# One expert layer in bf16 on one core: all of x loaded in float32 by SyncE and cast on chip

## The chip, the cores and the metric

The kernel runs on one NeuronCore of a Trainium2 chip. The core has five engines with instruction streams of their own: TensorE (PE, matmuls), VectorE (DVE), ScalarE (ACT), GpSimd (POOL, called Pool here) and SyncE (SP). [...] Data moves between the device memory and the on-chip SBUF by 16 DMA engines, which serve transfers that SyncE or Pool has issued. The metric is the device time of one execution in microseconds (us); lower is better.

## The reference

```python
n_experts, capacity, hidden, expert_hidden = 8, 256, 512, 2048

def reference(x, w1, w2):          # all float32
    h = np.matmul(x, w1)           # (8,256,512) @ (8,512,2048)
    h = np.maximum(h, 0)
    return np.matmul(h, w2).astype(np.float32)   # (8,256,2048) @ (8,2048,512)
```

Eight experts, each with its own tokens and weights: two matmuls with a ReLU between them. x is 4.19 MB, w1 and w2 are 33.55 MB each in float32.

## The kernel before, in words

**Data.** Weights are cast to bf16 by the DMA transfers that load them, into four slots each of `w1_sb` and `w2_sb` (slot = expert modulo 4). x is kept in bf16 in `x_sb`, which is the place of slot 2 of `w2_sb`: 16 rows of 512 elements per partition (`R` = 16, `H` = 512). TensorE turns it into `xT` by 64 transposes, and only then may the weights of slot 2 be loaded there.

**Order.** The kernel uses a Tile context only for its beginning. There, in a critical section (L135), SyncE issues one float32 transfer of the first four rows of x (`HEAD` = 4, L136) into the output buffer `out_sb`, which is free until the first expert is done. Then the context is closed (L137) and compiled, and everything after it is written out engine by engine with waits on the kernel's own semaphores:

- SyncE (L140 to L149) waits for each weight load in turn and counts it for TensorE (`c_w1`, `c_w2`). At the end it stores the last expert's output (L145).
- Pool (L152 to L201) issues the other twelve rows of x as one casting transfer (L153), makes the identity for the transposes (L154, L157), then issues all weight loads (L190): experts 0 and 1 of w1, the same of w2, experts 2 and 3 of w1, and so on. From the fourth on, each waits until its slot has been used; the fourth, w2 of experts 2 and 3, waits for all transposes (L171). A small output transfer (L181) goes ahead of the last half load of weights, and the output of experts 0 to 6 is issued behind the weights (L193).
- VectorE (L212 to L228) waits for the head of x (`d_head`), casts it into `x_sb` (L214), then moves half of the transposes from PSUM to `xT` (L206) and later the outputs from PSUM to `out_sb` (L225).
- ScalarE (L231 to L245) moves the other half of the transposes (L206), applies the ReLU (L239) and evicts the last output block (L245).
- TensorE waits for the cast, the identity and the rest of x (L323 to L325), runs the transposes (L328) and then a loop over the eight experts (L444): 64 matmuls into `h_ps`, in which each expert first takes its w1 count (L410), then 32 into `o_ps`, which take the w2 counts in two halves (L414). The helper of L99 takes a count, and all matmuls stand on L275.

The waits and the order of the lines are written by hand; no scheduler moves them.

Of the kernel before, what the change touches and what calls it, by code (L numbers as in the profile page):

```python
# [16 lines left out]
def kernel(  # L17
# [7 lines left out]
    nc = tc.nc  # L25
    P = 128
    E, C, H = x.shape
    F = w1.shape[2]
    MC = C // P
# [2 lines left out]

    R = E * C // P

    HEAD = 4

    NS = 4

# [10 lines left out]
    x_v = x.rearrange("e (pp r) k -> (e pp) (r k)", r=R)  # L49
# [7 lines left out]
    def allot(name, shape, dtype):  # L57
        nonlocal free
        places[name] = free
        t = nc.alloc_sbuf_tensor_at(name, shape, dtype, offset=free)  # L60
        free += math.prod(shape[1:]) * mybir.dt.size(dtype)
        return t


    out_sb = allot("out_sb", [P, E, MC, H], FP32)
# [7 lines left out]
    x_sb = w2_sb[:, 2, :]  # L73
# [8 lines left out]
    def sem(name):  # L82
        s = nc.alloc_semaphore(name)
        sems.append(s)
        return s

    d_last, d_pool = sem("d_last"), sem("d_pool")
# [3 lines left out]
        for w, slots in [(1, (0, 2, 3)), (2, (0, 1, 2, 3))]  # L91
        for i in slots
    }
    d_head, d_half = sem("d_head"), sem("d_half")
    s_event, s_cast, s_stored = sem("s_event"), sem("s_cast"), sem("s_stored")
    s_pe, v_last = sem("s_pe"), sem("v_last")

# [3 lines left out]
    def after_transposes(n):  # L101
        return s_pe, n

    def after_hidden(e, groups):
        return s_pe, K1 * MC + e * (NG + MC) + groups

    def after_outputs(e, halves):
        return s_pe, K1 * MC + e * (NG + MC) + NG + halves
# [22 lines left out]

    x_head = out_sb[:, :HEAD // MC].rearrange("p e m h -> p (e m h)")
    with tc.tile_critical(no_gpsimd_drain=True):  # L135
        nc.sync.dma_start(x_head, x_v[:, :HEAD * H]).then_inc(d_head, 16)  # L136
    tc.close()  # L137
    tc.compile()  # L138

# [1 line left out]
    for i, (w, es, h, n) in enumerate(loads):  # L141
# [8 lines left out]


    pool = nc.gpsimd  # L152
    pool.dma_start(x_sb[:, HEAD * H:], x_v[:, HEAD * H:]).then_inc(d_pool, 16)  # L153
    pool.memset(identity[:], 0.0).then_inc(s_event)  # L154
    pool.wait_ge(s_event, 1)

# [6 lines left out]
        pattern=[[-1, P]],  # L163
        channel_multiplier=1,
    ).then_inc(s_event)
    for i, (w, es, h, n) in enumerate(loads):


        old = es[-1] - NS
        if w == 2 and 2 in es:  # L170
            pool.wait_ge(*after_transposes(K1 * MC))  # L171
        if old >= 0 and h == 0:
            if w == 1:
                pool.wait_ge(*after_hidden(old, NG))
            else:
                pool.wait_ge(*after_outputs(old, MC))
        if i == len(loads) - 1:


            pool.wait_ge(s_event, 3)  # L180
            pool.dma_start(  # L181
                out_v[:16, 0, :16], out_sb[:16, 0, 0, :16]
            ).then_inc(d_pool, 16)
        e, ne, at_slot = es[0], len(es), es[0] % NS
        if w == 2:
            src = w2_v[:, e:e + ne, h:h + n, :].rearrange("p e h n -> p e (h n)")
            dst = w2_sb[:, at_slot:at_slot + ne, h * JH * H:(h + n) * JH * H]
        else:
            src, dst = w1_v[:, e:e + ne, :], w1_sb[:, at_slot:at_slot + ne, :]
        pool.dma_start(dst, src).then_inc(landed[i][0], 16)  # L190
    pool.wait_ge(s_event, 4)
    pool.wait_ge(d_pool, 32)
    pool.dma_start(  # L193
        out_v[:, :E - 1, :], out_sb[:, :E - 1].rearrange("p e m h -> p e (m h)")
    ).then_inc(d_pool, 16)
    pool.wait_ge(s_stored, 1)
    pool.wait_ge(d_pool, 48)
    used = [s.num for s in sems[1:]]
    used = range(min(used), max(used) + 1)
    pool.dma_reset(used)  # L200
# [9 lines left out]


    dve = nc.vector  # L212
    dve.wait_ge(d_head, 16)
    dve.tensor_copy(x_sb[:, :HEAD * H], x_head).then_inc(s_cast)  # L214
    dve.sem_inc(c_xt[0], 1)
    for ko in range(K1):
        dve.wait_ge(*after_transposes(ko * MC + 1))
# [11 lines left out]


    act = nc.scalar  # L231
    act.sem_inc(c_xt[1], 1)
    for ko in range(K1):
        act.wait_ge(*after_transposes(ko * MC + 2))
# [15 lines left out]
    pe = nc.tensor  # L250
# [42 lines left out]
    def last_column(step):  # L293

        return (P - 1) * step * 2
# [24 lines left out]
                i += 1  # L320
            t.then_inc(s_pe)

    pe.wait_ge(s_cast, 1)  # L323
    pe.wait_ge(s_event, 2)
    pe.wait_ge(d_pool, 16)  # L325
    x_first = X_AT + last_column(K1)
    pe.reg_mov(reg["x"], x_first)
    loop("transposes", reg["x"], x_first + K1 * 2, transposes)  # L328
# [146 lines left out]
```

## Time and profile before

| what | us |
|---|---|
| median of 3 runs | 179.47 |
| lowest and highest run | 179.31, 180.14 |
| the profiled execution's own time | 180.34 |
| its span, from the first to the last instruction | 179.0 |
| busy in that span: TensorE matmuls | 126.7 |
| ScalarE, VectorE, Pool | 38.7, 15.8, 10.9 |

The profile is of one execution. A timeline row has the start, the duration, the engine, the line, the operation with the tiles it writes and reads, and in brackets the idle time before it with what ended it; "q" behind an engine is its sequencer, which waits and issues transfers. A row of the stretches has the stretch, its length, the busy time of TensorE matmuls, TensorE weight loads, VectorE, ScalarE and Pool with counts, the granted clock, the share of the 16 DMA engines, and the GB/s written; a packet counts where it starts.
The queue that Pool issues to is called q0 (software_dynamic), SyncE's is q1 (hardware_dynamic).

### The profile page before, as it was taken

Reading aid. Unit: us, or ns where it says so; the run is one execution under the profiler, and the core shown is the slowest. Engines: PE = TensorE matmul, PEld = TensorE weight load, DVE = VectorE, ACT = ScalarE, POOL = GpSimd, SP = SyncE. Lnnn points to the kernel's source line nnn. Section 1 sums busy time; section 2 is a strip of 40 time slices with the busy share of each in tenths; the row PEclk is TensorE's granted clock in tenths of the full one; section 3 lists DMA queues with packets and bytes.
Section 4 is the critical chain, followed back from the end, with each engine's and each line's share of the span. In section 5 each row is a group of like instructions: output and inputs, shape, how many; then the busy total and the mean of one; then the engine's idle time right before and its main releaser. Section 6 shows DMA issues by size and latency. Waiting matters only on the chain. (4 is left out here: it accounts for less than half of the span.)

```text
span 179.0 us, 2075 instructions
## 1 busy us (share of the span) xinstructions
PE 126.7 (71%) x824; PEld 89.7 (50%) x832; DVE 15.8 (9%) x20; ACT 38.7 (22%) x38; POOL 10.9 (6%) x21
## 2 busy tenths in 40 slices
PE   0007630695029999993059999999999999959980
PEld 0006520585014695593023795695596497449530
DVE  0203420000000200200000200200110020020010
ACT  2002420044000063044000062053044044005310
POOL 3600010000000002101000101100020000001000
PEclk9999999999557999999657999999999999999999
DMA  5999989999999999999999998999999999999997
GB/s 185 253 207 231 227 190 231 227 194 223 231 209 205 227 216 201 231 216 198 231 220 194 231 223 190 231 227 194 223 231 205 209 234 216 198 212 218 303 421 310
DMA packets 3744, 40.37 MB, mean 226 GB/s; under 512 B 288, under 2 KB 288, under 8 KB 1312
## 3 DMA queue, kind: packets, MB, share of 16 engines
q0 software_dynamic: 3456, 38.80, 97.5%
q1 hardware_dynamic: 288, 1.57, 2.4%
HBM read 71.30 MB, written 4.20 MB: 422 GB/s over the span
## 5 line engine op out<-in xcount | busy, mean ns | idle before, releaser
L275 PE MATMUL o_ps<-w_sb,hT 128*128 x248 | 59.8, 396 | 19.6 <-PEq L99 18.8
L275 PE MATMUL h_ps<-xT,w_sb 128*128 x512 | 60.9, 281 | 11.3 <-PEq L99 11.3
L275 PEld LDWEIGHTS h_ps<-xT,w_sb 128*128 x512 | 57.7, 146 | 15.4 <-issue 12.0
L239 ACT ACTIVATE hT<-h_ps 128x1024 bf16<-128x1024 f32 x32 | 32.8, 1024 | 110.2 <-PE h_ps L275 110.2
L275 PEld LDWEIGHTS o_ps<-w_sb,hT 128*128 128x128 bf16 x256 | 25.5, 101 | 51.2 <-issue 24.7
L225 DVE COPY out_sb<-o_ps 128x512 f32<-128x512 f32 x15 | 9.7, 686 | 140.3 <-PE o_ps L275 140.3
L275 PE MATMUL xt_ps<-identity,w_sb 128*128 128x128 bf16 x64 | 7.6, 311 | 16.2 <-PEq L99 16.2
L275 PEld LDWEIGHTS xt_ps<-identity,w_sb 128*128 x64 | 6.5, 146 | 16.9 <-issue 16.9
L190 POOL DMA_DIRECT2D w_sb<-in_w_dram x12 | 8.0, 667 | 104.2 <-PE h_ps L275 56.9
L206 ACT COPY xT<-xt_ps 128x1024 bf16<-128x1024 bf16 x4 | 4.0, 1012 | 17.0 <-PE xt_ps L275 17.0
L206 DVE COPY xT<-xt_ps 128x1024 bf16<-128x1024 bf16 x4 | 4.9, 1224 | 12.2 <-PE xt_ps L275 12.2
L193 POOL DMA_DIRECT2D out_dram<-out_sb x1 | 1.0, 964 | 33.2 <-DMA out_dram<-out_sb 33.2
L245 ACT COPY out_sb<-o_ps 128x512 f32<-128x512 f32 x1 | 0.6, 586 | 5.9 <-PE o_ps L275 5.9
L206 ACT ACT_TABLE_LOAD x1 | 1.3, 1283 | 2.4 <-PEq L138 2.4
L214 DVE CAST w_sb<-out_sb 128x2048 bf16<-128x2048 f32 x1 | 1.2, 1227 | 5.8 <-DMA out_sb<-in_x_dram 5.8
L181 POOL DMA_DIRECT2D out_dram<-out_sb x1 | 0.5, 512 | 14.7 <-DVEq L228 14.7
L153 POOL DMA_DIRECT2D w_sb<-in_x_dram x1 | 0.7, 682 | 2.4 <-POOLq L138 2.4
L157 POOL TENSOR_SCALAR_AFFINE_SELECT identity<-identity 128x128 bf16<-128x128 bf16 x1 | 0.3, 284 | 0.2 <-POOL identity L154 0.2
L154 POOL MEMSET identity<- 128x128 bf16 x1 | 0.2, 224 | 0.0
L459 POOL MEMSET const-float32-0.0<- 128x1 f32 x1 | 0.1, 93 | 0.2 <-issue 0.2
L459 POOL MEMSET const-bfloat16-1.0<- 128x1 bf16 x1 | 0.1, 96 | 0.0
L459 POOL MEMSET const-uint8-127<- 128x1 uint8 x1 | 0.1, 96 | 0.0
(1 smaller groups left out, 0.1 us busy)
## 6 DMA issues: line engine op xcount, KB each, us to landing
w_sb<-in_w_dram POOLq DMA_DIRECT2D x5, 4096.0 KB, 47.1
w_sb<-in_w_dram POOLq DMA_DIRECT2D x5, 2048.0 KB, 51.2
out_dram<-out_sb POOLq DMA_DIRECT2D x1, 3584.0 KB, 12.9
w_sb<-in_w_dram POOLq DMA_DIRECT2D x2, 1024.0 KB, 43.3
w_sb<-in_x_dram POOLq DMA_DIRECT2D x1, 1536.0 KB, 10.6
out_sb<-in_x_dram SPq DMA_DIRECT2D x1, 1024.0 KB, 4.9
out_dram<-out_sb SPq DMA_DIRECT2D x1, 512.0 KB, 4.7
out_dram<-out_sb POOLq DMA_DIRECT2D x1, 1.0 KB, 33.7
```

The lines of the kernel that those rows point to most:

```text
L153: pool.dma_start(x_sb[:, HEAD * H:], x_v[:, HEAD * H:]).then_inc(d_pool, 16)
L157: pool.affine_select(out=identity[:], in_=identity[:], compare_op=mybir.AluOpType.not_equal, fill=1.0, base=0, pattern=[[-1, P]], channel_ ...
L181: pool.dma_start(out_v[:16, 0, :16], out_sb[:16, 0, 0, :16]).then_inc(d_pool, 16)
L190: pool.dma_start(dst, src).then_inc(landed[i][0], 16)
L193: pool.dma_start(out_v[:, :E - 1, :], out_sb[:, :E - 1].rearrange("p e m h -> p e (m h)")).then_inc(d_pool, 16)
L206: return copy(xT[:, ko, m].rearrange("k (ep r2) -> k ep r2", r2=R // MC), xt_ps[m][:].rearrange("k r2 ep -> k ep r2"),)
L214: dve.tensor_copy(x_sb[:, :HEAD * H], x_head).then_inc(s_cast)
L225: cp = dve.tensor_copy(out_sb[:, e, m, :], o_ps[m][:])
L239: act.activation(hT[:, g * GJ:(g + 1) * GJ, :].rearrange("p a c -> p (a c)"), h_ps[g % UG][:], mybir.ActivationFunctionType.Relu,).then_in ...
L245: act.copy(out_sb[:, E - 1, 1, :], o_ps[1][:]).then_inc(v_last)
L275: return pe.add_instruction(inst)
L459: nc = _bacc.Bacc("TRN2", target_bir_lowering=False, num_devices=1)
```

## The change

Three transfers by SyncE, of rows 0 to 3, 4 to 9 and 10 to 15, bring all of x in float32 into `out_sb`. They stand in the Tile context without a critical section, and each is put on the context's list of instructions that get none of its own semaphores. Each has a semaphore of the kernel, `d_x[0]` to `d_x[2]`. VectorE casts rows 0 to 3, 4 to 9 and 10 to 13, each when it has landed; ScalarE casts rows 14 and 15; TensorE waits for all four casts. Pool no longer loads x; its first weight load waits for `d_x[1]`, the first ten rows. Counts on `d_pool` at the end become one transfer smaller.

```diff
--- before.py
+++ after.py
@@ -32,7 +32,7 @@
 
     R = E * C // P
 
-    HEAD = 4
+    HEAD, BODY = 4, 10
 
     NS = 4
 
@@ -91,7 +91,7 @@
         for w, slots in [(1, (0, 2, 3)), (2, (0, 1, 2, 3))]
         for i in slots
     }
-    d_head, d_half = sem("d_head"), sem("d_half")
+    d_x, d_half = [sem(f"d_x{i}") for i in range(3)], sem("d_half")
     s_event, s_cast, s_stored = sem("s_event"), sem("s_cast"), sem("s_stored")
     s_pe, v_last = sem("s_pe"), sem("v_last")
 
@@ -131,9 +131,16 @@
 
 
 
-    x_head = out_sb[:, :HEAD // MC].rearrange("p e m h -> p (e m h)")
-    with tc.tile_critical(no_gpsimd_drain=True):
-        nc.sync.dma_start(x_head, x_v[:, :HEAD * H]).then_inc(d_head, 16)
+
+    x_f32 = out_sb[:].rearrange("p e m h -> p (e m h)")
+
+    def rows(a, b):
+        return slice(a * H, b * H)
+
+
+    for i, (a, b) in enumerate([(0, HEAD), (HEAD, BODY), (BODY, R)]):
+        load = nc.sync.dma_start(x_f32[:, rows(a, b)], x_v[:, rows(a, b)]).then_inc(d_x[i], 16)
+        tc.info.no_tile_sem_insts.add(load.ins.name)
     tc.close()
     tc.compile()
 
@@ -150,7 +157,6 @@
 
 
     pool = nc.gpsimd
-    pool.dma_start(x_sb[:, HEAD * H:], x_v[:, HEAD * H:]).then_inc(d_pool, 16)
     pool.memset(identity[:], 0.0).then_inc(s_event)
     pool.wait_ge(s_event, 1)
 
@@ -163,6 +169,7 @@
         pattern=[[-1, P]],
         channel_multiplier=1,
     ).then_inc(s_event)
+    pool.wait_ge(d_x[1], 16)
     for i, (w, es, h, n) in enumerate(loads):
 
 
@@ -189,12 +196,12 @@
             src, dst = w1_v[:, e:e + ne, :], w1_sb[:, at_slot:at_slot + ne, :]
         pool.dma_start(dst, src).then_inc(landed[i][0], 16)
     pool.wait_ge(s_event, 4)
-    pool.wait_ge(d_pool, 32)
+    pool.wait_ge(d_pool, 16)
     pool.dma_start(
         out_v[:, :E - 1, :], out_sb[:, :E - 1].rearrange("p e m h -> p e (m h)")
     ).then_inc(d_pool, 16)
     pool.wait_ge(s_stored, 1)
-    pool.wait_ge(d_pool, 48)
+    pool.wait_ge(d_pool, 32)
     used = [s.num for s in sems[1:]]
     used = range(min(used), max(used) + 1)
     pool.dma_reset(used)
@@ -210,8 +217,17 @@
 
 
     dve = nc.vector
-    dve.wait_ge(d_head, 16)
-    dve.tensor_copy(x_sb[:, :HEAD * H], x_head).then_inc(s_cast)
+    SPLIT = 14
+
+    def cast(copy, a, b):
+        return copy(x_sb[:, rows(a, b)], x_f32[:, rows(a, b)])
+
+    dve.wait_ge(d_x[0], 16)
+    cast(dve.tensor_copy, 0, HEAD).then_inc(s_cast)
+    dve.wait_ge(d_x[1], 16)
+    cast(dve.tensor_copy, HEAD, BODY).then_inc(s_cast)
+    dve.wait_ge(d_x[2], 16)
+    cast(dve.tensor_copy, BODY, SPLIT).then_inc(s_cast)
     dve.sem_inc(c_xt[0], 1)
     for ko in range(K1):
         dve.wait_ge(*after_transposes(ko * MC + 1))
@@ -229,6 +245,8 @@
 
 
     act = nc.scalar
+    act.wait_ge(d_x[2], 16)
+    cast(act.copy, SPLIT, R).then_inc(s_cast)
     act.sem_inc(c_xt[1], 1)
     for ko in range(K1):
         act.wait_ge(*after_transposes(ko * MC + 2))
@@ -320,9 +338,8 @@
                 i += 1
             t.then_inc(s_pe)
 
-    pe.wait_ge(s_cast, 1)
     pe.wait_ge(s_event, 2)
-    pe.wait_ge(d_pool, 16)
+    pe.wait_ge(s_cast, 4)
     x_first = X_AT + last_column(K1)
     pe.reg_mov(reg["x"], x_first)
     loop("transposes", reg["x"], x_first + K1 * 2, transposes)
```

## What was predicted, before the changed kernel was run

> **What bounds the kernel now.** I read the page first: its second and third parts, for which resource is never idle.
>
> ```profile
> span 179.0 us, 2075 instructions
> DMA  5999989999999999999999998999999999999997
> GB/s 185 253 207 231 227 190 231 227 194 223 231 209 205 227 216 201 231 216 198 231 220 194 231 223 190 231 227 194 223 231 205 209 234 216 198 212 218 303 421 310
> q0 software_dynamic: 3456, 38.80, 97.5%
> q1 hardware_dynamic: 288, 1.57, 2.4%
> ```
>
> The sixteen DMA engines are full from the first slice to the last (each slice is 4.5 us). Pool's queue (q0) takes 97.5% of them, SyncE's (q1) 2.4%. TensorE cannot be the bound where it waits for weights, so next the timeline, for its waits and the end:
>
> ```profile
> 32.93 9.89 PE L275 MATMUL h_ps<-xT,w_sb 128*128 x64 [9.21 <-PEq L99]
> 159.41 7.31 PE L275 MATMUL h_ps<-xT,w_sb 128*128 x64 [2.08 <-PEq L99]
> 166.61 7.07 PE L275 MATMUL o_ps<-w_sb,hT 128*128 x31
> 173.71 0.59 ACT L245 COPY out_sb<-o_ps 128x512 f32<-128x512 f32 x1 [5.93 <-PE o_ps L275]
> 174.32 0.35 SPq L145 DMA_DIRECT2D out_dram<-out_sb  x1
> ```
>
> Line 99 is TensorE taking a count that SyncE gives when a weight load has landed. TensorE stands 9.21 us before its first weights, and again 2.08 us before the last expert's. From there the rest is fixed work: 14.3 us of matmuls to 173.7, the eviction, the last store. So the end moves with the stream of weights one for one, and the stream moves with the moment at which x is through the DMA engines. Anything that TensorE does before 32.93 has 9.21 us of cover. The change is therefore worth what it does to the stretch ahead of the weights. That stretch, from the timeline, with one row of a narrower timeline for Pool's third weight issue and the page's times to landing:
>
> ```profile
> 0.35 0.10 POOL L459 MEMSET const-uint8-127<- 128x1 uint8 x1
> 0.95 0.38 SPq L136 DMA_DIRECT2D out_sb<-in_x_dram  x1
> 2.83 0.68 POOL L153 DMA_DIRECT2D w_sb<-in_x_dram  x1 [2.38 <-POOLq L138]
> 4.41 2.80 POOL L190 DMA_DIRECT2D w_sb<-in_w_dram  x3 [0.15 <-issue]
> 5.83 1.23 DVE L214 CAST w_sb<-out_sb 128x2048 bf16<-128x2048 f32 x1 [5.83 <-DMA out_sb<-in_x_dram]
> 13.95 1.89 PE L275 MATMUL xt_ps<-identity,w_sb 128*128 128x128 bf16 x16 [13.95 <-PEq L99]
> 24.03 0.72 POOL L190 DMA_DIRECT2D w_sb<-in_w_dram  x1 [16.82 <-PE xt_ps L275]
> ```
>
> ```profile
> 5.87 1.33 POOL L190 DMA_DIRECT2D w_sb<-in_w_dram  x1
> ```
>
> ```profile
> w_sb<-in_x_dram POOLq DMA_DIRECT2D x1, 1536.0 KB, 10.6
> out_sb<-in_x_dram SPq DMA_DIRECT2D x1, 1024.0 KB, 4.9
> ```
>
> And its DMA rates by stretch (last two columns: share of the DMA engines, GB/s written), then two answers on single stretches: the weights from 12.2 to 167.6 us, and the big float32 store from 173 to 175.4 us:
>
> ```profile
> 1.00:2.00 1.00, 0.00 (x0) 0.00 (x0) 0.00 (x0) 0.00 (x0) 0.00 (x0) 1.00 0.10 16
> 2.00:3.00 1.00, 0.00 (x0) 0.00 (x0) 0.00 (x0) 0.59 (x1) 0.17 (x1) 1.00 0.86 197
> 3.00:4.00 1.00, 0.00 (x0) 0.00 (x0) 0.00 (x0) 0.69 (x1) 0.76 (x3) 1.00 0.99 418
> 4.00:5.00 1.00, 0.00 (x0) 0.00 (x0) 0.00 (x0) 0.00 (x0) 0.85 (x2) 1.00 1.16 438
> 11.00:12.00 1.00, 0.00 (x0) 0.00 (x0) 0.00 (x0) 0.00 (x0) 0.00 (x0) 1.00 0.93 197
> 12.00:13.00 1.00, 0.00 (x0) 0.00 (x0) 0.00 (x0) 0.00 (x0) 0.00 (x0) 1.00 1.29 270
> ```
>
> ```profile
> DMA packets 2399, 33.55 MB, mean 216 GB/s; under 512 B 224, under 2 KB 224, under 8 KB 224
> ```
>
> ```profile
> DMA packets 249, 1.02 MB, mean 425 GB/s; under 512 B 0, under 2 KB 0, under 8 KB 249
> ```
>
> The lesson is in the last two: a transfer that casts float32 to bf16 writes 216 GB/s, so it reads 432; a plain float32 one moves 425. The engines pay for the float32 side either way.
>
> **The change, part by part.** x has 1,048,576 elements, 4.19 MB in float32, in 16 rows per partition.
>
> *Twelve rows leave Pool's casting transfer for SyncE's float32 ones.* Before, they write 1.57 MB: 1.57 / 0.216 = 7.28 us of the DMA engines. After, they move 3.15 MB: 3.15 / 0.425 = 7.40 us. Price +0.12 us. Bounds: at the 438 of the 4:5 row 7.18 us (-0.10), at its neighbour's 418 7.53 us (+0.25).
>
> *SyncE issues outside a section.* It now does so at 0.95 us, after the section's entry. Every engine is held at a start-up barrier that cannot end before Pool's last constant memset (0.35 + 0.10 = 0.45). Without the section the first issue falls between 0.45 and 0.95; I take 0.75, since the barrier's own signals stay: -0.20 us (bounds -0.50 and 0). The second and third issue cost SyncE 0.38 us each, while the first transfer is still moving. They also delay the end-of-context barrier, where Pool, VectorE and ScalarE arrive, by less than a microsecond; Pool's identity is not used until the transposes.
>
> *When x is through.* The rows 1:2 to 4:5 hold 1.07 MB by 5.0 us, so by 4.8 after the change. The other 3.12 MB at 425 take 7.35 us: the last packets start at about 12.15. Before, the same count gives 5.0 + 1.55 / 0.216 = 12.2.
>
> *Pool's weights wait for ten rows (d_x[1]).* This is the new wait. All weight loads stand behind it in Pool's queue; before, the first three were issued from 4.41 to 7.21, some 5 us ahead of need. Ten rows are 2.62 MB: 1.55 MB beyond the 1.07, 3.65 us, so 8.45. From the end of the bytes to the semaphore the head needed 5.83 - 5.0 = 0.83 us, so the wait ends at 9.3. VectorE starts at the same moment, on the same semaphore, its second cast: 3072 columns at 1.23 us for 2048 make 1.84 us, to 11.15. What that does to Pool is in the rows: the first two weight issues take from 4.41 to 5.87, 0.73 each; the third, issued while the cast runs, takes 1.33 and ends at 7.20, which is 0.14 after the cast's end at 7.06. So I let Pool's first issue end 0.14 after the cast: 11.3, not 9.3 + 0.73 = 10.05.
>
> [...]
>
> From the end of an issue to the first packet I need the body of x: issued by 2.83 + 0.68 = 3.51. These rows are for 2.83 to 4.79 us, then 4.5 to 5.5:
>
> ```profile
> q1 hardware_dynamic: 99, 0.81, 98.5%
> ```
>
> ```profile
> q0 software_dynamic: 16, 0.20, 105.6%
> q1 hardware_dynamic: 42, 0.21, 51.1%
> ```
>
> Pool's packets appear at 4.8, as SyncE's run out: at most 1.3 us after the issue's end, and perhaps much less, since they may have stood behind the head. So the first weight packets come between 11.3 and 12.6, where x runs out at 12.15. The gap in the stream is 0 to 0.45 us. I take 0, the value that the handover at 4.8 is nearest to. If Pool cannot begin its issue at all until the cast ends, it is 11.15 + 0.73 + 1.3 = 13.2, a gap of up to 1.05.
>
> *Casts and transposes.* The last rows land at 12.15 + 0.83 = 13.0; VectorE casts four rows (1.23 us) beside ScalarE's two, so TensorE may begin 0.5 us after 14.2, at about 14.7 instead of 13.95. Transposes end, and Pool's fourth weight issue goes, 0.8 us later than 24.03. The cover is the 9.21 us before 32.93, and three loads of 4 MB already queued. Price 0; gone only if x landed some 8 us later still. The casts stand on engines that do nothing else then.
>
> *Waits renumbered at the end, one fewer Pool transfer*: no work on the path.
>
> **The sum:** -0.20 + 0.12 + 0 = -0.08 us. The profiled execution took 180.34 us, its span 179.0; the median of the runs is 179.47. The difference applies to each, so 179.4 us.
>
> **The rivals.**
>
> *The cast starves Pool's descriptors, and the DMA engines run dry between x and the weights.* This one ends slower. It decides when the first weight packet comes after 12.15; every 0.1 us beyond goes into the time. At the bound from rows, 13.2, the sum is -0.08 + 1.05 = +0.97: 180.4 us; half-way, 179.9. For it: Pool's third issue was stretched by 0.6 us by a cast a third shorter. Against: x's last 1.5 MB cover 3.7 us of the wait.
>
> *Each of SyncE's transfers starts slowly, as the first did.* Row 2:3 moved 197 where 425 was possible: 0.54 us lost. Twice more is +1.1: 180.5 us. Against it: the head handed over to the body within 4.5 to 5.5, and the body to the weights within 11 to 13, without such a dip, though those were other queues. [...]
>
> *The weights' packets mix with the last part of x.* Then x lands later, up to some microseconds, and the transposes with it. The bytes are the same and the cover holds: 179.4 us. For it: two queues with work at once. Against it, from 174.3 to 176 us, after SyncE's store was issued at 174.32:
>
> ```profile
> q0 software_dynamic: 176, 0.72, 102.9%
> ```
>
> No packet of SyncE's is among them, so a queue that is deep may go first.
>
> *The change does not bring SyncE's issue forward*, because something other than the section holds it at 0.95: +0.12, 179.6 us.
>
> **How the numbers follow.** A measurement of this kernel can tell about 0.5%, 0.9 us, from no change: faster means under 178.6, slower over 180.4. Chances: forecast 0.58; starved Pool 0.16, of which 0.06 at its upper end or beyond; slow starts 0.08, nearly all of it slower; mixed queues 0.12; no earlier start 0.06. A gain of 0.9 would need more than every favourable bound: -0.50 - 0.10 = -0.60 us. I leave it 0.05 out of the forecast's share. So faster 0.05, same 0.81, slower 0.14. Range: low at 179.47 - 0.60, 178.8 with the rounding of a median whose runs differ by some tenths; high at the starved bound, 180.4.
>
> **What would show it.** SyncE's first issue at 0.7 to 0.8. Windows at 418 to 438 GB/s from 3 to 12 us, then falling to about 216 without a dip: a window under 190 around 12 is the starved Pool, one near 6 or 9 the slow starts. Pool's first weight issue beginning near 9.3 and lasting about 2 us, ending just behind VectorE's cast. Transposes from about 14.7; later than 16 is mixed queues. TensorE's wait ahead of its first weights shorter by a microsecond, its first h_ps matmul at about 32.9. The forecast is wrong if that matmul stands more than 0.9 us from 32.93, or if TensorE no longer waits ahead of the last expert.

## The result, and the profile after

The changed kernel takes 180.72 us (six runs, 180.30 to 180.94) where the kernel before, run beside it, took 179.66. The ratio is 1.0052, 95% interval 1.0032 to 1.0072: slower by 0.5%, where 179.4 us and no measurable change had been forecast. A repeat on one chip, below, gave 1.0041 (1.0026 to 1.0056).

The two profiles alone do not show it. The page after, first lines and queues:

```profile
span 179.0 us, 2072 instructions
DMA  5999999999999999999999999999999999999997
GB/s 207 431 362 223 194 216 234 201 220 223 223 201 220 231 198 216 234 201 220 223 216 205 223 231 198 216 231 205 212 231 216 205 223 227 194 214 218 301 422 306
q0 software_dynamic: 3312, 37.23, 93.3%
q1 hardware_dynamic: 576, 4.72, 6.5%
```

The span is 179.0 us in both. But this execution, 180.30 us, is the fastest of the six, and the execution of the kernel before that the prediction worked from, 180.34 us, lies above all twelve of its runs in the repeat (179.44 to 180.16). A page is one draw. So the stages have to be compared. The start, from the timeline after (four rows of the start, then TensorE's waits for weights and the end):

```profile
0.74 1.33 SPq L142 DMA_DIRECT2D out_sb<-in_x_dram  x3
9.21 1.76 DVE L223 CAST w_sb<-out_sb 128x3072 bf16<-128x3072 f32 x1 [2.47 <-DMA out_sb<-in_x_dram]
9.48 3.06 POOL L197 DMA_DIRECT2D w_sb<-in_w_dram  x3 [5.89 <-DMA out_sb<-in_x_dram]
14.68 1.89 PE L293 MATMUL xt_ps<-identity,w_sb 128*128 128x128 bf16 x16 [14.68 <-PEq L99]
...
24.75 0.72 POOL L197 DMA_DIRECT2D w_sb<-in_w_dram  x1 [12.21 <-PE xt_ps L293]
...
33.46 9.23 PE L293 MATMUL h_ps<-xT,w_sb 128*128 x64 [9.01 <-PEq L99]
52.79 0.58 PE L293 MATMUL o_ps<-w_sb,hT 128*128 x1 [10.10 <-PEq L99]
...
159.29 8.86 PE L293 MATMUL h_ps<-xT,w_sb 128*128 x64 [2.33 <-PEq L99]
168.03 7.07 PE L293 MATMUL o_ps<-w_sb,hT 128*128 x31
175.75 0.35 SPq L152 DMA_DIRECT2D out_dram<-out_sb  x1
```

SyncE's issue, the casts, Pool's issue and the start of the transposes stand where they were forecast. The first weights, though, are there at 33.46, not 32.93, and the transposes have nothing to do with it: TensorE waited 9.01 us. The DMA rates of two stretches after, then the second stretch before (last columns: DMA share, GB/s):

```profile
3.00:12.00 9.00, 0.00 (x0) 0.00 (x0) 2.99 (x2) 1.15 (x1) 2.87 (x5) 1.00 1.03 435
12.00:15.00 3.00, 0.32 (x4) 0.33 (x5) 1.23 (x1) 1.04 (x1) 0.54 (x1) 1.00 1.04 190
```

```profile
12.00:15.00 3.00, 1.05 (x11) 1.06 (x11) 0.00 (x0) 0.00 (x0) 0.00 (x0) 1.00 1.07 227
```

x comes in at 435 GB/s without a dip. Then, where the DMA engines go over from x to the weights, 190 GB/s are started instead of 227: (227 - 190) x 3 = 111 KB, 0.5 us at the weights' 216. The share of the DMA engines stays above 1 in both (1.04 and 1.07): they are not idle in the mean, their packets take longer, as their durations, further below, show.

**The handover, engine by engine.** In the trace before, SyncE's two transfers leave 32 packets of 4 bytes and Pool's fifteen leave 240: 16 for each transfer, as many as there are DMA engines. Every transfer also adds 16 times to its semaphore. I read these as one for each engine, at the end of its share. A load counts as landed with the last of them: TensorE's first h_ps matmul starts 0.17 us after it, before (32.76, 32.93) and after (33.29, 33.46). The times of these additions are in the trace. The table has, for every kernel of this study, the end of Pool's first issue, the ends of SyncE's last x packets, Pool's first packet, the additions for the first weight load (first and last engine), the start of the first o_ps matmul, and the span of the profiled execution.

| kernel | issue ends | x ends | first Pool packet | first load lands | first o_ps | span | ratio of times |
|---|---|---|---|---|---|---|---|
| before, as first shown | 3.51 (x) | 4.80 to 5.46 | 4.80 | 31.90 to 32.76 | 52.46 | 179.0 | |
| before, repeat | 3.51 (x) | 4.84 to 5.33 | about 4.8 | 31.82 to 32.52 | 52.05 | 178.3 | 1.0008 |
| after | 11.11 | 11.96 to 12.48 | 11.96 | 32.04 to 33.29 | 52.79 | 179.0 | 1.0052 |
| after, repeat | 11.07 | 12.02 to 12.42 | 12.02 | 32.22 to 32.86 | 52.44 | 179.0 | 1.0041 |
| before, no section | 3.09 (x) | 4.58 to 5.13 | about 4.6 | 31.74 to 32.82 | 52.48 | 179.1 | 1.0023 |
| after, section back | 11.35 | 12.25 to 12.76 | 12.26 | 32.52 to 34.13 | 53.69 | 180.0 | 1.0076 |
| wait for 4 rows | 6.88 | mixed | 9.98 | 31.72 to 32.14 | 51.70 | 178.0 | 0.9963 |
| no wait | 4.67 | mixed | 7.85 | 31.78 to 32.21 | 51.79 | 177.8 | 0.9961 |
| second cast on ScalarE | 10.31 | 12.10 to 12.46 | 12.12 | 32.44 to 33.82 | 53.38 | 179.4 | 1.0048 |
| wait for all 16 rows | 14.24 | 12.03 to 12.46 | 14.95 | 35.16 to 35.67 | 55.22 | 181.3 | 1.0150 |
| wait for 8 rows | 9.22 | 12.21 to 12.60 | 12.21 | 31.93 to 32.66 | 52.14 | 178.5 | 0.9965 |
| wait for 6 rows | 7.91 | mixed | 11.14 | 31.79 to 32.22 | 51.71 | 177.8 | 0.9965 |
| later issues held | 11.27 | 12.08 to 12.58 | 12.09 | 32.17 to 33.45 | 52.97 | 179.1 | 1.0045 |
| first load split | 11.12 | 11.95 to 12.52 | 11.95 | 32.28 to 33.78 (its second half) | 53.25 | 179.4 | 1.0049 |
| before, head of 8 | 3.51 (x) | mixed | 7.02 | 32.21 to 32.51 | 52.05 | 178.1 | 0.9983 |
| before, head of 8, no section | 3.09 (x) | mixed | 6.32 | 31.80 to 32.32 | 51.84 | 178.0 | 0.9971 |

"(x)" marks the kernels whose first Pool transfer is a part of x; "mixed" that Pool's packets came before SyncE's last. Two readings. First, span minus the start of the first o_ps matmul lies between 126.0 and 126.6 us in all sixteen traces: but for up to 0.6 us, what these kernels gain or lose is made ahead of 52 us. Second, the time goes with the last engine rather than with the mean: span minus the last addition for the first load (the second half where it is split) lies between 145.6 and 146.3 us in the sixteen traces, span minus the mean addition between 145.8 and 147.0. In the first pair of traces the changed kernel's first engine is 0.1 us later than before, its last one 0.5. In the repeat all engines are later alike, the first by 0.40 us and the last by 0.34. There 0.7 us of span are lost, and the rest of them appears only at the end: for the last half load of weights the first and the last addition lie 1.1 us apart, after about 0.7 in the loads before it. Why they part there is open.

### The profile page after: what moved, and what is told of

It is laid out like the page before. It is cut to its first block, busy times and chain, and to the rows that moved or that the text cites. A ratio compares the mean times of both kernels' runs of the same rounds, so it can differ in the third digit from the quotient of the medians.

```text
span 179.0 us, 2072 instructions
## 1 busy us (share of the span) xinstructions
PE 128.2 (72%) x824; PEld 90.4 (51%) x832; DVE 18.8 (11%) x22; ACT 39.7 (22%) x39; POOL 10.4 (6%) x20
## 5 line engine op out<-in xcount | busy, mean ns | idle before, releaser
L293 PE MATMUL o_ps<-w_sb,hT 128*128 x248 | 60.5, 400 | 18.7 <-PEq L99 17.9
L293 PE MATMUL h_ps<-xT,w_sb 128*128 x512 | 61.8, 284 | 11.3 <-PEq L99 11.3
L293 PEld LDWEIGHTS h_ps<-xT,w_sb 128*128 x512 | 58.3, 146 | 15.7 <-issue 12.0
L223 DVE CAST w_sb<-out_sb 128x2048 bf16<-128x2048 f32 (+1 forms) x3 | 4.2, 1405 | 9.9 <-DMA out_sb<-in_x_dram 9.9
L223 ACT CAST w_sb<-out_sb 128x1024 bf16<-128x1024 f32 x1 | 1.0, 1045 | 8.7 <-DMA out_sb<-in_x_dram 8.7
L188 POOL DMA_DIRECT2D out_dram<-out_sb x1 | 0.5, 512 | 14.7 <-DVEq L244 14.7
```

Of the source, the lines that this page charges most:

```text
L188: pool.dma_start(out_v[:16, 0, :16], out_sb[:16, 0, 0, :16]).then_inc(d_pool, 16)
L223: return copy(x_sb[:, rows(a, b)], x_f32[:, rows(a, b)])
L293: return pe.add_instruction(inst)
```

## The experiments

**Both kernels again, and two parts of the change alone.** My first theory was that TensorE's clock, not the weights, made the difference, since in the profile after the last expert's first matmuls took 8.86 us instead of 7.31. The granted clock (second last but one column) after:

```profile
159.30:160.60 1.30, 1.30 (x12) 1.30 (x13) 0.00 (x0) 0.00 (x0) 0.00 (x0) 1.00 1.05 221
160.60:164.00 3.40, 3.40 (x18) 2.72 (x17) 0.00 (x0) 1.02 (x1) 0.00 (x0) 0.50 1.02 210
```

*The kernel before, unchanged:*

> The kernel before, unchanged, against itself. It gives the spans and clocks of several executions, of which only one was shown. Theory clock (the changed kernel's weights are not later, but TensorE's granted clock drops to half ahead of or in the last expert in more of its executions): ratio 1.000 within 0.002, spans of 178.0 to 178.8 with few executions that drop at the end. Theory x (the float32 x phase makes the weights later by 1 us, and the two profiles shown happen to hide it): the same ratio, but spans spread no more than 0.4 us around one value.

179.83 us (twelve runs), ratio 1.0008 (0.9995 to 1.0020), spans from 178.1 to 178.8. The profiled one has the same half clock in its last expert (8.84 us for the h_ps matmuls), yet its span, 178.3, is the shorter one. The clock falls as the cause. The store that ends the kernel is issued at 175.12 here and was at 174.32 in the first trace, and still the span is 0.7 us shorter. Its first packet came at 176.44 there, 2.1 us after the issue began, and all but 16 of Pool's 896 output packets had started; in the profile after it came at 176.60, 0.85 us after, behind all but 9. By these times the 4.2 MB of output in the DMA engines set the end, and they hide TensorE's 1.5 us.

*The changed kernel, unchanged:*

> The changed kernel, unchanged, again. Both theories: ratio about 1.005. Theory clock: first w1 landing within 0.3 us of 33.3 in this trace too, weights' end within 0.3 us of 168, and a half-clock stretch between 157 and 167. Theory x: weights' end at 168.5 or later. Theory chance (the six and six runs drew badly): ratio 1.000 to 1.002.

180.42 us, ratio 1.0041. Again a half clock, but in this trace too the weights are later (table). Theory chance falls.

*The kernel before without the section:*

```diff
-    with tc.tile_critical(no_gpsimd_drain=True):
-        nc.sync.dma_start(x_head, ...).then_inc(d_head, 16)
+    load = nc.sync.dma_start(x_head, ...).then_inc(d_head, 16)
+    tc.info.no_tile_sem_insts.add(load.ins.name)
```

> The kernel before with one part of the change: the head of x is issued by SyncE without the critical section; the body stays Pool's casting transfer, ahead of the weights. Theory clock: the stream is 0.2 us earlier; time -0.2 us unless the earlier start alone moves the clock's drop, then up to +1. Theory x: -0.2 us (ratio 0.999), since the body is still cast by the transfer. A rival, the section's removal itself costs: ratio 1.005.

180.18 us, ratio 1.0023 (1.0011 to 1.0034). SyncE issues at 0.74, the first engine's weights are 0.1 us earlier, the last engine's 0.3 later than in the repeat of before. So an earlier start alone can be lost again; in this trace the spread of the engines loses it. The rival that the section's removal itself costs had 1.005; the loss is half of that, and the last experiment returns to it.

*The changed kernel with the section back:*

```diff
+    with tc.tile_critical(no_gpsimd_drain=True):
         for i, (a, b) in enumerate([(0, HEAD), (HEAD, BODY), (BODY, R)]):
```

> The changed kernel with the critical section put back around its three transfers, so that only the section part is undone: SyncE issues at 0.95 again. Theory x: the change's loss plus 0.2 us, ratio 1.006. Theory clock: the transposes move another 0.2 us, ratio 1.003 to 1.007. If the section's removal is what costs: ratio 1.000.

181.32 us, ratio 1.0076 (1.0055 to 1.0097), above all forecasts: 0.9 us over the changed kernel for a start that is 0.2 us later. The rest is again spread: 1.6 us between first and last engine. That pointed at the handover from SyncE's queue to Pool's.

**When Pool issues.** Four kernels change only what the first weight issue waits for, or what stretches it.

*Four rows instead of ten:*

```diff
-    pool.wait_ge(d_x[1], 16)
+    pool.wait_ge(d_x[0], 16)
```

> The changed kernel, Pool's weights wait for the first four rows of x (d_x[0]) instead of ten: Pool's first issue begins near 5.7 and ends near 7, five microseconds before x is through. Theory late descriptors (the stretched issue ends at 11.1, only 0.9 us before x runs out, and the 16 DMA engines start on the weights slowly and unevenly because of it): the loss goes, first h_ps matmul near 32.6, ratio 0.998 to 1.001. Theory switch (an engine that goes from SyncE's queue to Pool's pays 0.4 to 0.6 us however early Pool issued): ratio 1.003 to 1.005 as with the change. Theory mixing: weights' packets come between x's, transposes start at 16 or later, time as in one of the other two.

179.13 us, ratio 0.9963 (0.9944 to 0.9981). Pool's first issue lasts from 5.78 to 6.88. Queues from 6.88 to 9.97 us, then from 9.97 to 12:

```profile
q1 hardware_dynamic: 123, 1.31, 99.8%
```

```profile
q0 software_dynamic: 22, 0.36, 83.0%
q1 hardware_dynamic: 23, 0.28, 33.2%
```

For 3.1 us after the issue no packet of Pool's moves. Then both queues take turns, 22 packets to 23, and every engine's first weight packet takes 1.23 us, as later ones do. Packets of 12 KB of x and of 16 KB of weights come in turns: up to 11 us Pool's sixteen, in the microsecond after that sixteen of SyncE's and six of Pool's. For the 3.1 us ahead of that, with 123 packets of SyncE's alone, no run shows what holds Pool's. x is complete only at 20.05, the transposes start here:

```profile
21.84 1.89 PE L293 MATMUL xt_ps<-identity,w_sb 128*128 128x128 bf16 x16 [21.84 <-PEq L99]
...
51.70 0.58 PE L293 MATMUL o_ps<-w_sb,hT 128*128 x1 [9.20 <-PEq L99]
```

They end near 31.6, and the first h_ps matmul starts at 33.34, 1.2 us after the last addition for its weights and later than forecast. But TensorE then waits 9.20 us for w2, so nothing was lost. The gain over the kernel before, 0.4%, is more than any of the theories had allowed; the kernel with a head of eight rows, below, shows where part of it comes from.

*No wait at all* (the same line taken out):

> The changed kernel without Pool's wait: the weights are issued from about 3.7 us, right behind the identity, as in the kernel before. No transfer writes what another reads, so nothing is unordered. Theory late descriptors: as with the wait for four rows, ratio 0.998 to 1.001. Theory switch: 1.003 to 1.005. Theory mixing: more of it than with the wait for four rows, transposes at 20 or later and part of the 9 us cover used, but time as in one of the other two.

179.20 us, ratio 0.9961 (0.9944 to 0.9979). Issue ends at 4.67, first packet at 7.85: 3.2 us. The first transposes move to 29.20, beyond what I had expected, and the first h_ps matmul to 40.70. Here the 9 us of cover are used up, but TensorE catches up before it has to wait for w2.

*The second cast on ScalarE:*

```diff
-    dve.wait_ge(d_x[1], 16)
-    cast(dve.tensor_copy, HEAD, BODY).then_inc(s_cast)
...
+    act.wait_ge(d_x[1], 16)
+    cast(act.copy, HEAD, BODY).then_inc(s_cast)
     act.wait_ge(d_x[2], 16)
```

> The changed kernel with the second cast (rows 4 to 9) on ScalarE instead of VectorE, at the same place; the wait for ten rows stays. If VectorE's cast is what stretches Pool's first issue, that takes 0.75 us instead of 1.64 and ends near 10.2, 0.9 us earlier; if not, 1.64 again. Theory late descriptors with the cast as cause: ratio 0.999 to 1.002. Theory late descriptors, 0.9 us not enough, or theory switch: 1.003 to 1.005.

180.89 us, ratio 1.0048 (1.0027 to 1.0070). Groups of this kernel around 9.5 us, then of the changed kernel, Pool alone:

```profile
L223 ACT CAST w_sb<-out_sb 128x3072 bf16<-128x3072 f32 x1 | 2.8, 2751 | 5.0 <-DMA out_sb<-in_x_dram 5.0
L197 POOL DMA_DIRECT2D w_sb<-in_w_dram x1 | 0.9, 867 | 5.9 <-DMA out_sb<-in_x_dram 5.9
```

```profile
L197 POOL DMA_DIRECT2D w_sb<-in_w_dram x1 | 1.6, 1635 | 5.9 <-DMA out_sb<-in_x_dram 5.9
```

VectorE's cast does stretch Pool's issue, 1635 ns beside it and 867 without, as the prediction had it. But to end the issue 0.8 us sooner bought nothing. The handover is even more ragged: 164 GB/s in the three microseconds, against 227 before and 190 with the change:

```profile
12.00:15.00 3.00, 0.35 (x4) 0.36 (x5) 1.23 (x1) 1.05 (x1) 0.00 (x0) 1.00 1.01 164
```

*All sixteen rows:*

```diff
-    pool.wait_ge(d_x[1], 16)
+    pool.wait_ge(d_x[2], 16)
```

> The changed kernel, Pool's weights wait for all of x (d_x[2], near 12.85). The DMA engines must run dry, which measures what an issue needs until its first packet and how long the first packets take. Theory late descriptors: first issue beside VectorE's last cast, from 13.1 to 14.3, first packet 0.5 to 1.3 us later, at 14.8 to 15.6; ratio 1.015 to 1.022 over the kernel before. Theory switch with an empty engine to start on: the first packets as slow as with the change (1.3 to 2.1 us) on top of the gap. If the first packet comes sooner than 0.5 us after the issue ends, descriptors were not late with the change either.

182.62 us, ratio 1.0150 (1.0105 to 1.0196). This measures an issue to idle engines; its time fits both theories. Pool's issue, then the rates from 12.5 to 14.9 and after:

```profile
13.14 1.10 POOL L197 DMA_DIRECT2D w_sb<-in_w_dram  x1 [9.56 <-DMA out_sb<-in_x_dram]
```

```profile
12.50:14.90 2.40, 0.24 (x3) 0.24 (x4) 1.23 (x1) 1.04 (x1) 1.76 (x2) 1.00 0.00 0
14.90:15.90 1.00, 1.00 (x12) 1.00 (x10) 0.16 (x1) 0.00 (x0) 0.77 (x2) 1.00 1.81 262
```

The issue ends at 14.24, the first packet comes at 14.95, 0.7 us later. The first sixteen packets take 1.54 to 2.08 us each in the trace where later ones take 1.23. In the changed kernel most of the first ones take 1.3 to 1.9: slow in the same way, though there the mean engine gets its first one only 0.2 us after its last x packet. Such slow first packets are called cold below; what makes them slow no run shows.

**Where the edge lies.** By now the theory was *lead*: while SyncE's packets are under way, Pool's first one comes some 3.1 us after its issue has ended; an engine that runs out of SyncE's sooner starts cold, and some start late, each to a different degree. Its rival, *switch*: every handover costs, and only a long mix hides it.

*Eight rows, and six rows* (a fourth transfer, n = 8 or 6; casts unchanged):

```diff
-    ... enumerate([(0, HEAD), (HEAD, BODY), (BODY, R)]):
+    ... enumerate([(0, HEAD), (HEAD, n), (n, BODY), (BODY, R)]):
```

> The changed kernel with its second transfer cut in two (rows 4 to 7 and 8 to 9), Pool's weights waiting for eight rows; casts as in the changed kernel. Pool's first issue then begins near 8.2, ahead of the second cast, and ends near 9, 3 us before x is through. Theory lead (with SyncE's packets under way it takes about 3.1 us from the end of Pool's issue to its first packet, and an engine that runs out of SyncE's packets sooner starts on the weights cold): at the edge, first o_ps matmul 51.7 to 52.3, ratio 0.997 to 1.001. Theory switch (any handover costs, only a long mix of both queues hides it): 52.5 to 53.3, ratio 1.003 to 1.005.

179.44 us, ratio 0.9965 (0.9945 to 0.9986). The issue ends 3.0 us ahead of the first engine's last x packet and Pool's first packet comes at 12.21, just as x ends. On two engines a Pool packet already goes ahead of the small write that counts x. Eleven of the sixteen first weight packets take 1.23 us: nearly the same moment of handover as in the changed kernel, but for most engines no cold start.

> As with eight rows, but the second transfer is cut at row 6 and Pool waits for six rows: its first issue ends near 7.8, 4.2 us before x is through. Theory lead: no loss, first o_ps matmul near 51.7, ratio 0.995 to 0.998, weights' packets from about 10.9 and transposes at 18 to 20. Theory switch: mixing is short, so a loss of 0.3 to 0.7 us is left, ratio 0.999 to 1.003.

179.18 us, ratio 0.9965 (0.9944 to 0.9985). Queues from 7.91, the end of the issue, to 11.13:

```profile
q1 hardware_dynamic: 140, 1.41, 102.8%
```

First packet at 11.14, 3.2 us after the issue; all first weight packets take 1.23 us, and the engines' spread is 0.43 us. Transposes from 19.55. Both first o_ps matmuls stand where lead put them; the ratio with eight rows is a hair better than its range. Switch falls: it allowed neither time.

*Pool's second and third issue later* (a wait for `d_x[2]` ahead of the second load):

> The changed kernel; only Pool's second and third weight issues are later, behind a wait for all of x (d_x[2]), so that Pool writes nothing while the DMA engines go over from x to the weights. If Pool's next issues disturb the handover, the loss goes: first o_ps matmul 51.9 to 52.2, ratio 0.998 to 1.001. Theories lead and switch: as with the change, 52.4 to 53.4, ratio 1.003 to 1.006.

180.42 us, ratio 1.0045 (1.0022 to 1.0068), first o_ps matmul at 52.97. Pool's later issues are not what disturbs the handover.

**The handover of the kernel before.** Two doubts were left: the size of Pool's first transfer, and that in the kernel before Pool's body, too, went out only 1.3 us ahead of the end of SyncE's head.

*The first load split* (w1 of expert 0 and of expert 1 as two loads):

> The changed kernel with Pool's first weight load (w1 of experts 0 and 1) cut into one per expert; the wait for ten rows and the lead stay. Theory lead: the loss stays, first o_ps matmul 52.4 to 53.4, ratio 1.003 to 1.006. Theory size (a pair's 256 descriptors make the handover dear): first o_ps matmul near 52.0, ratio 0.998 to 1.001.

180.62 us, ratio 1.0049 (1.0030 to 1.0068), first o_ps matmul at 53.25. In the trace after, the ten loads of 4 and 2 MB make 1920 packets of 16 KB, so 256 for a pair and 128 for half of one. The size of the first transfer is not the cause.

*A head of eight rows:*

```diff
-    HEAD = 4
+    HEAD = 8
```

> The kernel before with one constant changed: SyncE's head of x has 8 rows instead of 4, Pool's casting body the other 8. Pool's body issue still ends near 3.5, and SyncE's packets last until about 7.4, so the lead is 3.8 us instead of 1.3. Theory lead: the kernel before loses at this handover too; the ragged start goes, first o_ps matmul 51.8 to 52.1, ratio 0.996 to 0.998. If the handover of the kernel before costs nothing: ratio 1.000.

179.42 us, ratio 0.9983 (0.9972 to 0.9995). Queues from 3.51, where Pool's issue of the body ends, to 7.0, then from 7.0 to 8.8:

```profile
q1 hardware_dynamic: 87, 1.43, 96.3%
```

```profile
q0 software_dynamic: 32, 0.26, 69.9%
q1 hardware_dynamic: 16, 0.26, 34.7%
```

3.5 us of silence here, then turns, with 32 packets of 8 KB to 16 of 16 KB in the 1.8 us. The first o_ps matmul, 52.05, is where lead put it; the gain, 0.17%, is a little under its forecast. The ten runs lie between 179.38 and 179.54, those of before, run beside them, between 179.27 and 180.46. So the kernel before had a ragged handover too, which cost it part of its time and, by these runs, most of its scatter.

*The same without the section:*

> As with a head of 8 rows, and the head issued without the critical section, so 0.2 us earlier. Theory lead: leaving out the section was slower with four rows only through the ragged handover; here it is 0.2 us faster than with the section, ratio 0.995 to 0.997. If the section's removal costs by itself: ratio 0.998 to 1.001.

179.26 us, ratio 0.9971 (0.9955 to 0.9986), between the two forecasts: 0.16 us under the one with the section. With this handover the section's removal is worth about its earlier start, so it does not cost by itself. In the kernel with four rows it was lost, there with a spread of 1.1 us.

## Why the prediction was wrong

- **SyncE's issue at 0.75:** 0.74. Right.
- **Float32 costs no more than the cast:** 435 GB/s from 3 to 12 us, x through at 11.96 to 12.48 for 12.15. Right; the rival of slow starts falls.
- **Pool's issue from 9.3 to 11.3, held by VectorE's cast:** 9.48 to 11.11, which is 0.14 us behind the cast's end at 10.97, and 867 instead of 1635 ns when the cast is taken away. Right.
- **A gap of 0 where Pool's weights take over from x:** this step failed. The first packet itself came as forecast, at 11.96, 0.85 us after the issue's end and just as the first engine ran out of x. What the first packets cost was put at nothing, because at the handover at 4.8 of the kernel before no window dipped. There the sixteen first packets of the body start as SyncE's end, and take 0.1 us more than later ones in the mean. In the changed kernel the first weight packets start 0.2 us after the end of x in the mean (0.1 in the repeat) and take 0.4 to 0.5 us more than 1.23: half a microsecond for each engine, and more for some. The cure shows the cause: with an issue that ends about 3 us or more ahead of the end of x (four, six, eight rows, no wait) the loss is gone; with 0.8 us more of lead it is not.
- **"At most 1.3 us after the issue's end, and perhaps much less":** one row could not bound this. It holds where SyncE's packets run out; while they last, the way is 3.0 to 3.5 us (six kernels). The rows shown held a sign of it: SyncE's last store, issued by 174.67, has its first packet at 176.44, 1.8 us later and behind all but 16 of Pool's 896 output packets.
- **The sum over all engines:** windows of all sixteen can't show that a load waits for the last. The mean addition for the first load moved by 0.31 us from before to after, the last engine by 0.53; in the repeat by 0.35 and 0.34. That is about half of the 0.6 to 1.1 us between the medians. Both traces of the changed kernel are of its fastest execution; where the rest arises, but for the 0.4 us at the end of the repeat, is open.
- **Transposes later at no price:** 14.68 for 14.7, Pool's fourth issue at 24.75, hidden. Right, and with room: even 29.20 cost nothing.
- **The end moves with the stream:** right, within the 126.0 to 126.6 us, though not for the reason given. What ties them is the 4.2 MB of output behind the weights rather than TensorE's 14.3 us: with the half clock at 160.6 the last store is issued 1.4 us later than before, and its first packet comes 0.2 us later.
- **The rival that Pool is starved** had the place and the sign, at 179.9 to 180.4 us, and its mark, a window under 190 GB/s, came (98 from 13 to 14 us, behind 242). But it had the wrong lever: without VectorE's cast beside the issue it is as slow (1.0048). No run shows descriptors; what the cast stretches, by the runs, is the issue (1635 ns for 867). **Mixed queues**, which I priced as neutral, are the cure.

The two signs of a wrong forecast did not come: the first h_ps matmul moved 0.53 us, under the 0.9 allowed, and TensorE still waits ahead of the last expert. The bound was too wide for a loss of this size. Against its own trace the sum of -0.08 us looks right, as the spans are equal; that is luck, for that trace was a late draw of the kernel before. Not settled: what the DMA engines do in the 3 us, why first packets are slow, why a lead between 0.9 and 1.8 us leaves some engines up to a microsecond late and others not, and why the section put back made the spread so much wider.

## What to carry to other kernels

Here Pool's queue took the DMA engines over from SyncE's without a loss where its first issue ended 3 us or more ahead of SyncE's last packets; a wait that delayed it to "just in time", 0.85 us ahead, cost 0.4 to 0.8%. Where one queue follows another in your kernel, try the first issue earlier, and measure the lead that it needs there. Read such a handover by its last engine, not by a mean rate alone. And before comparing two profiles, see where each stands among its kernel's runs. The change with Pool waiting for four rows, 179.13 us, is faster than the kernel before and the changed one, by 0.4% and about 0.8%.

## What the runs showed of the hardware

While SyncE's packets lasted, Pool's first packet came 3.0 to 3.5 us after its issue ended, whether the issue ended at 3.1, 3.5, 4.7, 6.9, 7.9 or 9.2 us. Where they ran out sooner it came with their end, 0.85 us after the issue in the changed kernel, and on idle engines 0.7 us after it. Where both queues had packets, they took turns: 22 to 23 in the kernel that waits for four rows. The first weight packets of 16 KB took 1.5 to 2.1 us on idle engines and mostly 1.3 to 1.9 in the changed kernel; where the queues took turns they took 1.23, like later ones. VectorE's cast beside Pool's first issue made that 1635 ns long, where it took 867 beside ScalarE's. The spread between the sixteen engines that such a start makes stays: it is 1.6 us with the section back and 0.3 with a head of eight rows, in the first weight load as in the loads 120 us later. At the very end it grew in some traces, most in the changed kernel's repeat, from 0.7 to 1.1.
